# Squares of a head's rotated channels join its other channels before the statistics matmuls of a two-layer hybrid trunk

## The chip, the cores and the metric

The kernel runs on one core of a Trainium2 chip. The metric is device time in microseconds (us) of one execution. Before the change it took 756.54 us, the median of three runs (756.30, 756.54 and 756.56 us). One further execution was recorded by the hardware profiler; all durations below come from it.

A core has five engines with a queue each, and every queue runs in order: TensorE (PE, matrix products; its weight loads are shown as PEld), VectorE (DVE), ScalarE (ACT), GpSimd (POOL) and SyncE (SP, which here issues nearly all DMAs). Engines wait for each other through semaphores.

## The reference

Two layers. Each normalizes the residual stream, projects it, runs a causal pooling mixer and a latent attention side by side, and adds both back. The lines that matter here are the normalizations (D_MODEL 1024, 512 tokens behind 16 meta tokens, so 528 in all; 8 heads with 64 plain and 32 rotated channels):

```python
def rmsnorm(x, gain):
    xf = x.astype(jnp.float32)
    inv = lax.rsqrt(jnp.mean(xf * xf, axis=-1, keepdims=True) + NORM_EPS)
    return (xf * inv * gain.astype(jnp.float32)).astype(x.dtype)

def mla(c_q_raw, c_kv_raw, k_rope_raw, pos, ...):
    c_q = rmsnorm(c_q_raw, g_qa)
    c_kv = rmsnorm(c_kv_raw, g_kva)
    q = (c_q @ w_q_b).reshape(B, L, N_HEADS, QK_HEAD_DIM)
    ...
    k = jnp.concatenate([k_nope, k_pe], axis=-1)
    q = rmsnorm(q, g_qn)
    k = rmsnorm(k, g_kn)
    q = jnp.concatenate([q[..., :64], apply_rope(q[..., 64:], pos)], axis=-1)
    k = jnp.concatenate([k[..., :64], apply_rope(k[..., 64:], pos)], axis=-1)
    o = causal_block_attention(q, k, v)

# in each layer
    h = rmsnorm(h_res, norm_gain[l])
    proj = h @ w_in[l]          # u, z, c_q, c_kv, k_rope, z_mla, g_pool, g_mla
```

So each layer needs the sum of squares of a token over the 1024 channels of the stream, over the 256 channels of `c_kv`, and, for every head, over the 96 channels of its query and of its key.

## The kernel before

Activations lie transposed: channels on the 128 partitions, tokens along the free axis. FULL is the two halves of 264 tokens; the last layer works on the 512 real tokens (XTOK) where it can, so its products are 512 wide. Every f32 product is made of three matmuls (`mm3`, lines 205 to 207: high by high, high by low, low by high), with weights split into a high part on ACT (`whi`, line 200) and a low part on DVE (`wlo`, line 201). Three weight buffers rotate. The projections form one list of products, the main stream; a Python clock (`clk`, nanoseconds of matmul columns) says where in this stream the rest of the program is written: `fill_now(ns)` writes about so many nanoseconds of main stream first. A scheduler then sets the final order on each engine. PE runs what stands in its queue in order, so the main stream is the cover for all that the other engines do.

Sums over channels, which lie on partitions, are matmuls with a thin stationary operand. Two places make them:

- `norm_sums` (line 426): squares of `c_kv` (tiles `csq`, two of 128 channels) and, in the second layer, squares of the stream (tiles `xsq`, eight, already added on POOL to two by `square_x`, line 382) against a 128x32 block of ones. Each matmul uses a quarter of the array's columns (`tile_position=(0, g)`, g = 0, 32, 64, 96), so four of them make one round. In the first layer the sums over the stream come from rows of `x` instead (line 400). The sums go by DMA to DRAM (line 438 or 440) and come back folded on 16 partitions (line 448); `newton` makes reciprocal square roots, which go out and come back spread over the partitions as `rinv` and `cinv` (line 465).
- `stat` and `stat_go` (line 535): squares of keys, queries, the shared rotated key (`kr_rest`) and an epsilon row (`acc`, C_CQ) against 128x16 selector columns of `cst`, which choose the head. All wait for the last square of the batch. Before, a layer has 24: 8 for keys, 2 for the rotated key, 2 for `acc`, 4 for the queries' rotated channels (`qr`, two tiles with the rotated channels of four heads each), 8 for the queries' other channels (`qn`, four tiles with two heads each). `stat_rows` (lines 543 and 544) evacuates, and `qk_stats` goes on to the factors of queries and keys, `kdr` in DRAM and the broadcasts `bc`, from which `keys` and `prep` build the operands of the heads' scores on POOL (lines 807, 809 and 811).

`q_stat` squares a half of a query tile on ACT (line 730) into a scratch half taken from `halves()`: parts of `xb`, then of `attD` and `attE`. `rope` (lines 573 to 576) rotates on DVE and POOL. `square_x` squares a tile of the new stream for the next layer.

Of the kernel before, what the change touches and what calls it, by code (L numbers as in the profile page):

```python
# [9 lines left out]
F32 = mybir.dt.float32  # L10
# [4 lines left out]
ALU = mybir.AluOpType  # L15
# [65 lines left out]
def trunk(ctx, tc, xT, xrow, mrow, pos, win, wkr, wqb, wkb, wvb, wgr, wpu, wmu, wout, gains, const, yT):  # L81
# [255 lines left out]
    scr = dp.tile([P, 8, SEQ], F32, name="scr")  # L337
    nsr = [dp.tile([4, T], F32, name=f"nsr{l}") for l in range(DEPTH)]
    ndr = [dp.tile([3, T], F32, name=f"ndr{l}") for l in range(DEPTH)]
# [8 lines left out]
    class Layer:  # L348
        def __init__(self, l):
            self.l, self.last = l, l == DEPTH - 1  # L350
            self.XS = XTOK if self.last else FULL
            self.x0 = NM if self.last else 0
            self.xt = xt if l == 0 else [None] * 8
            self.hs, self.us, self.zps = hbuf, [None] * 4, [None] * 4
            self.cs, self.cqs, self.ys, self.am = [None] * 2, [None] * 6, [None] * 4, [None] * 8
            self.kn, self.qn, self.zms, self.ogs = [None] * 4, [None] * 4, [None] * 4, [None] * 4
            self.qr, self.qf = [None] * 2, [None] * 2
            self.gms, self.mg, self.xr, self.vw = [None] * 8, [None] * 8, [None] * 8, []
            self.made = [None] * 8
            self.csq, self.xsq = [None] * 2, [None] * 8  # L360
            self.sq, self.half = [], halves()
            self.hosted = self.st = self.acc = self.inv = self.cinv = self.kraw = self.kp = None
# [13 lines left out]
        def square_x(self, k):  # L376
            self.xsq[k] = slot(f"cq{4 + k}" if k < 4 else f"q{k}")
            made = act.activation(self.xsq[k][:, :T], self.xt[k][:, :T], AF.Square)
            for w in (1, 2):
                if k % (2 * w) == 2 * w - 1:  # L380
                    d, e = self.xsq[k - 2 * w + 1], self.xsq[k + 1 - w]
                    gp.tensor_add(d[:, :T], d[:, :T], e[:, :T])
# [24 lines left out]
        def norm_sums(self):  # L407
            if self.l:
                fill_now(2600)
            else:  # L410
# [5 lines left out]
                for _ in range(9):  # L416
                    next(rows)
            px, pc = mmt() if self.l else None, mmt()
            xs = self.xsq[::4] if self.l else []
            runs = [(px, t, m, m < 2, m >= len(xs) - 2) for m, t in enumerate(xs)]  # L420
            runs += [(pc, t, m, True, True) for m, t in enumerate(self.csq)]
            for k in range(0, len(runs), 2):
                for s, (a, b) in enumerate(FULL):
                    for ps, t, m, start, stop in runs[k:k + 2]:
                        g = 64 * s + 32 * (m % 2)
                        mm = pe.matmul(ps[g:g + 32, :HALF], ones[:, 0:32], t[:, a:b], start=start, stop=stop,  # L426
                                       tile_position=(0, g))
                        if t is not self.csq[1]:
                            behind(mm, self.csq_last)
            self.kr_sums()  # L430
            sums = tmp()
            for s, (a, b) in enumerate(FULL):
                if self.l:
                    act.activation(sums[0:64, a:b], px[64 * s:64 * s + 64, :HALF], AF.Copy)
                dve.tensor_copy(sums[64:128, a:b], pc[64 * s:64 * s + 64, :HALF])
            raw, norms = nsr[self.l], ndr[self.l]
            if self.l:
                sp.dma_start(raw, sums[0:97:32, 0:T])
            else:
                sp.dma_start(raw[2:4], sums[64:97:32, 0:T])  # L440
# [5 lines left out]
            nq = sm.tile([16, 4, C], F32, tag="nq", name=nm("nq"))  # L446
# [3 lines left out]
            dve.scalar_tensor_tensor(out=na[:, 0, :], in0=nq[:, 1, :], scalar=1.0 / D, in1=na[:, 0, :],  # L450
                                     op0=ALU.mult, op1=ALU.add)
            dve.tensor_scalar(na[:, 1, :], na[:, 0, :], EPS, None, op0=ALU.mult)
            dve.tensor_scalar(ny[:, 2, :], na[:, 1, :], EPS, None, op0=ALU.mult)
            for m in range(2):
                dve.scalar_tensor_tensor(out=na[:, 1, :], in0=nq[:, 2 + m, :], scalar=1.0 / 256,
                                         in1=na[:, 1, :], op0=ALU.mult, op1=ALU.add)
            newton(ny[:, 0:2, :], na, nt)
# [266 lines left out]

        def q_stat(self, ps, a, b, c):
            for a0, b0 in FULL:
                a0, b0 = max(a, a0), min(b, b0)
                if a0 < b0:
                    q = next(self.half)
                    made = act.activation(q[:, :b0 - a0], ps[:, a0 - a:b0 - a], AF.Square)  # L730
                    self.stat(q[:, :b0 - a0], a0, b0, c, made)

        def ev_qr(self, r):
            def ev(ps, a, b):
                if a == self.x0:
                    self.qr[r] = (slot(f"q{4 + 2 * r}", F32R), slot(f"q{5 + 2 * r}", F32R))
                    self.qf[r] = slot(f"q{2 + r}")
                f = self.qf[r]
                act.activation(f[:, a:b], ps, AF.Copy, scale=self.g(G_QR))
                self.q_stat(ps, a, b, C_IR + 4 - 4 * r)  # L740

                self.rope(f[:, a:b], f[:, a:b], a, b)
                split(*self.qr[r], f[:, a:b], a, b)
            return ev

        def ev_qn(self, p):
            def ev(ps, a, b):
                if a == self.x0:
                    self.qn[p] = slot(f"q{p}")
                act.activation(self.qn[p][:, a:b], ps, AF.Copy, scale=self.g(G_QN))  # L750
                self.q_stat(ps, a, b, C_IK + 6 - 2 * p)
            return ev

        def qk_stats(self):
            fill_now(LAG + 100)
            self.stat_go()
# [36 lines left out]
        def prep(self, h):  # L793
            p, odd = h // 2, h % 2
            n0, r0 = (64, 0) if odd else (0, 64)
            kd = self.ks[p][odd]
            g0 = 32 * (h % 4)
            qh, ql = qhl[odd]
# [11 lines left out]
            for d, f in zip((qh, ql), self.qr[h // 4]):  # L810
                gp.tensor_copy(d[r0:r0 + 32, x0:T], f[g0:g0 + 32, x0:T])  # L811
            m = P if odd else QK
# [414 lines left out]
def constants():  # L1227
# [5 lines left out]
    c[64:128, C_IK + 15] = 1.0  # L1233
    for i in range(4):
        c[32 * i:32 * i + 32, C_IR + 12 + i] = 1.0
    c[0:32, C_KPE:C_KPE + 8] = 1.0
# [12 lines left out]
def arrange(x, positions, meta_tokens, norm_gain, w_in, pool_w_group, pool_scale, pool_w_up, q_a_norm_gain,  # L1249
# [16 lines left out]
    no, ro = np.arange(64), 64 + np.arange(32)  # L1266
    cols = np.concatenate([QK * h + ro for h in range(H)] + [QK * h + no for h in range(H)])
    wqb = tiles(w_q_b[:, :, cols])
# [27 lines left out]
```

## Time and profile before

| what | value |
|---|---|
| median of three runs | 756.54 us |
| the profiled execution | 756.64 us, with a span of 754.9 us from its first to its last instruction |
| granted TensorE clock | full in all 40 slices |
| PE busy | 749.7 us, 99% of the span |
| DVE, ACT, POOL busy | 548.1, 395.9 and 218.8 us |
| statistics matmuls, line 535 | 2.80 us of the chain in each layer, at 149.3 and 528.1 us |
| norm matmuls, line 426 | 0.58 us at 24.8 us and 1.03 us at 405.3 us |

A row of the timeline gives start, duration, engine, line, operation, output and inputs, shape and count, and in brackets the idle time before it with what ended it. Matmul rows overlap, since matmuls are pipelined: the distance between starts is what one costs. An f32 matmul of lines 426, 501 and 535 shows as two records, so 8 records are 4 matmuls.

### The profile page before, as it was taken

Reading aid. Unit: us, or ns where it says so; the run is one execution under the profiler, and the core shown is the slowest. Engines: PE = TensorE matmul, PEld = TensorE weight load, DVE = VectorE, ACT = ScalarE, POOL = GpSimd, SP = SyncE. Lnnn points to the kernel's source line nnn. Section 1 sums busy time; section 2 is a strip of 40 time slices with the busy share of each in tenths; the row PEclk is TensorE's granted clock in tenths of the full one; section 3 lists DMA queues with packets and bytes.
Section 4 is the critical chain, followed back from the end, with each engine's and each line's share of the span. In section 5 each row is a group of like instructions: output and inputs, shape, how many; then the busy total and the mean of one; then the engine's idle time right before and its main releaser. Section 6 shows DMA issues by size and latency. Waiting matters only on the chain.

```text
span 754.9 us, 14329 instructions
## 1 busy us (share of the span) xinstructions
PE 749.7 (99%) x5038; PEld 682.9 (90%) x5038; DVE 548.1 (73%) x1209; ACT 395.9 (52%) x866; POOL 218.8 (29%) x267
## 2 busy tenths in 40 slices
PE   9999999999999999999999999999999999999998
PEld 8999899999999999999997898887788888888887
DVE  5588777457999988684466477676478999975942
ACT  6755655645565665542355446456345666653321
POOL 1126404204463620061130264023044435111400
PEclk9999999999999999999999999999999999999999
DMA  8532223443765567525642322234447756773472
GB/s 316 162 108 89 74 82 86 113 116 119 211 186 166 151 194 192 156 86 157 183 145 85 114 84 66 89 90 120 108 135 210 190 156 181 195 200 93 127 227 84
DMA packets 72853, 106.58 MB, mean 141 GB/s; under 512 B 14102, under 2 KB 34966, under 8 KB 72780
## 3 DMA queue, kind: packets, MB, share of 16 engines
q1 hardware_dynamic: 72636, 105.39, 47.6%
q8 instruction: 40, 0.66, 0.4%
q14 instruction: 33, 0.27, 0.1%
q10 hardware_dynamic: 144, 0.26, 0.1%
HBM read 89.76 MB, written 15.86 MB: 140 GB/s over the span
## 4 chain that ended last, share of the span: by engine, by line
PE 98%; DMA 1%; ACT 0%; SPq 0%; issue 0%; DVE 0%; ACTq 0%
PE mm L205 29%; PE mm L207 29%; PE mm L206 29%; PE S L205 2%; PE S L207 2%; PE S L206 2%; PE o L980 1%; PE o L983 1%; PE S L535 1%; PE S L881 1%; DMA attE<-pdr 1%; PE S L501 0%; DMA xb<-xT 0%; PE mm L995 0%; PE mm L426 0%
## 5 line engine op out<-in xcount | busy, mean ns | idle before, releaser
L205 PE MATMUL mm<-hh,whi 128*128 128x264 f32 (+2 forms) x1072 | 336.1, 315 | 0.6 <-ACT whi L200 0.6
L206 PE MATMUL mm<-hl,whi 128*128 128x264 f32 (+2 forms) x1072 | 336.6, 315 | 0.0
L207 PE MATMUL mm<-hh,wlo 128*128 128x264 f32 (+2 forms) x1072 | 336.4, 316 | 0.0
L201 DVE TENSOR_TENSOR wlo<-raw,whi 128x512 fp32r<-128x512 f32 (+2 forms) x238 | 173.4, 730 | 95.8 <-ACT whi L200 92.4
L200 ACT ACTIVATE whi<-raw 128x512 fp32r<-128x512 f32 (+2 forms) x238 | 142.3, 600 | 176.1 <-PE mm L206 136.4
L205 PEld LDWEIGHTS mm<-hh,whi 128*128 128x128 f32 x1072 | 201.3, 188 | 15.0 <-issue 0.8
L206 PEld LDWEIGHTS mm<-hl,whi 128*128 128x128 f32 x1072 | 201.6, 188 | 12.9
L207 PEld LDWEIGHTS mm<-hh,wlo 128*128 128x128 f32 x1072 | 200.9, 188 | 12.3
L649 POOL TENSOR_TENSOR racc<-racc,tmp 128x264 f32<-128x264 f32 (+1 forms) x15 | 14.4, 959 | 132.3 <-ACT tmp L648 132.3
L1055 POOL TENSOR_TENSOR tmp<-tmp,xb 128x264 f32<-128x264 f32 (+1 forms) x24 | 27.0, 1137 | 49.1 <-DVE tmp L1053 46.4
L833 DVE CUSTOM_DVE_ANT_0 S<-S,maskw,nqs 128x240 f32<-128x240 f32 (+4 forms) x80 | 37.8, 492 | 4.2 <-PE S L207 3.9
L811 POOL CAST qhl<-q 32x528 fp32r<-32x528 f32 (+1 forms) x32 | 25.1, 800 | 44.2 <-PE S L881 42.9
L809 POOL CAST kh<-cq 32x528 fp32r<-32x528 f32 x16 | 15.6, 976 | 69.8 <-issue 36.1
L206 PE MATMUL mm<-th,whi 128*128 128x264 f32 (+1 forms) x108 | 34.7, 321 | 0.0
L205 PE MATMUL mm<-cq,whi 128*128 128x264 f32 (+1 forms) x108 | 34.7, 321 | 0.0
L205 PE MATMUL mm<-u,whi 128*128 128x264 f32 (+1 forms) x108 | 34.6, 321 | 0.0
L206 PE MATMUL mm<-cq,whi 128*128 128x264 f32 (+1 forms) x108 | 34.5, 321 | 0.0
L207 PE MATMUL mm<-cq,wlo 128*128 128x264 f32 (+1 forms) x108 | 34.5, 321 | 0.0
L207 PE MATMUL mm<-u,wlo 128*128 128x264 f32 (+1 forms) x108 | 34.5, 319 | 0.0
L959 DVE TENSOR_TENSOR attE<-attE,th 128x640 fp32r<-128x640 f32 x32 | 26.9, 862 | 3.7 <-ACT th L958 3.7
L840 ACT ACTIVATE cq<-S,bia 128x400 f32<-128x400 f32 (+2 forms) x48 | 24.4, 511 | 9.2 <-DVE bia L894 7.7
L843 POOL COPY pm<-cq 128x16 f32<-128x16 f32 x32 | 18.2, 570 | 37.7 <-ACT cq L840 37.5
(301 smaller groups left out, 1369.5 us busy)
## 6 DMA issues: line engine op xcount, KB each, us to landing
raw<-win SPq DMA_DIRECT2D x143, 256.0 KB, 3.2
pdr<-attD SPq DMA_DIRECT2D x16, 640.0 KB, 3.7
attE<-pdr SPq DMA_DIRECT2D x64, 160.0 KB, 3.9
raw<-wout SPq DMA_DIRECT2D x32, 256.0 KB, 2.8
raw<-wpu SPq DMA_DIRECT2D x16, 256.0 KB, 2.7
raw<-wmu SPq DMA_DIRECT2D x16, 256.0 KB, 2.7
raw<-wqb SPq DMA_DIRECT2D x12, 256.0 KB, 2.6
xb<-xT SPq DMA_DIRECT2D x8, 264.0 KB, 5.5
```

What stands on the lines that cost most here:

```text
L200: act.activation(hi[:, :n], raw[:, :n], AF.Copy)
L201: dve.tensor_sub(lo[:, :n], raw[:, :n], hi[:, :n].bitcast(F32))
L205: first = pe.matmul(out, wh, xh, start=start, stop=False)
L206: pe.matmul(out, wh, xl, start=False, stop=False)
L207: newest[0] = pe.matmul(out, wl, xh, start=False, stop=stop)
L809: gp.tensor_copy(d[r0:r0 + 32, :], f[g0:g0 + 32, :])
L811: gp.tensor_copy(d[r0:r0 + 32, x0:T], f[g0:g0 + 32, x0:T])
L833: return dve.tensor_tensor_reduce(out=sv, in0=sv, in1=mask, scale=nqs[:, i, h:h + 1], scalar=3e38, op0=ALU.add, op1=ALU.min, accum_out=bia ...
L840: act.activation(pv, sv, AF.Exp, scale=-1.0, bias=bia[:, i:i + 1], accum_out=rs[:, c:c + 1])
L843: gp.tensor_copy(pm[:, i, 16 * odd:16 * odd + 16], pt[i][:, 0:NM])
L959: dve.tensor_sub(got[:, a:b], f[:, a:b], hi[:, a:b].bitcast(F32))
L1055: gp.tensor_add(t[:, :b - a], t[:, :b - a], self.am[m][:, a:b])
```

## The change

- Queries: the squares of the rotated channels (`qr`) are kept (`rsq`) and get no matmul of their own. When a `qn` tile has been squared, the 32 partitions of each of its two heads get their head's rotated squares added, on POOL for the tiles 0 to 2 and on DVE for tile 3. So that the partitions match, the rotated channels of heads 1 and 2 of each four change places (`SEAT`), in the weights' columns and in `prep`.
- Keys and tokens: in `norm_sums` the two `c_kv` squares are added to one tile on POOL, and in the second layer the two tiles of the stream's squares too (in `square_x`, the step of width 4). One PSUM tile holds all sums, and DVE alone evacuates it. The DMA to DRAM and back has a row fewer in the first layer and two fewer in the second.
- The statistics are written 600 ns of main stream later: `fill_now(LAG + 700)`.

```diff
+SEAT = (0, 2, 1, 3)
...
     def square_x(self, k):
         made = act.activation(self.xsq[k][:, :T], self.xt[k][:, :T], AF.Square)
-            for w in (1, 2):
+            for w in (1, 2, 4):
                 if k % (2 * w) == 2 * w - 1:
                     d, e = self.xsq[k - 2 * w + 1], self.xsq[k + 1 - w]
                     gp.tensor_add(d[:, :T], d[:, :T], e[:, :T])
...
-            px, pc = mmt() if self.l else None, mmt()
-            xs = self.xsq[::4] if self.l else []
-            runs = [(px, t, m, m < 2, m >= len(xs) - 2) for m, t in enumerate(xs)]
-            runs += [(pc, t, m, True, True) for m, t in enumerate(self.csq)]
-            for k in range(0, len(runs), 2):
-                for s, (a, b) in enumerate(FULL):
-                    for ps, t, m, start, stop in runs[k:k + 2]:
-                        g = 64 * s + 32 * (m % 2)
...
+            ps, c = mmt(), self.csq[0]
+            self.csq_last = gp.tensor_add(c[:, :T], c[:, :T], self.csq[1][:, :T])
+            runs = [(self.xsq[0], 0)] * self.l + [(c, 32)]
+            for i, (a, b) in enumerate(FULL):
+                for t, m in runs:
+                    g = 64 * i + m
+                    mm = pe.matmul(ps[g:g + 32, :HALF], ones[:, 0:32], t[:, a:b], start=True, stop=True,
+                                   tile_position=(0, g))
+                    behind(mm, self.csq_last)
...
-                if self.l:
-                    act.activation(sums[0:64, a:b], px[64 * s:64 * s + 64, :HALF], AF.Copy)
-                dve.tensor_copy(sums[64:128, a:b], pc[64 * s:64 * s + 64, :HALF])
+                g = 0 if self.l else 32
+                dve.tensor_copy(sums[g:64, a:b], ps[64 * s + g:64 * s + 64, :HALF])
...
-        def q_stat(self, ps, a, b, c):
+        def q_stat(self, ps, a, b, p=None, r=None):
             for a0, b0 in FULL:
                 a0, b0 = max(a, a0), min(b, b0)
                 if a0 < b0:
-                    q = next(self.half)
-                    made = act.activation(q[:, :b0 - a0], ps[:, a0 - a:b0 - a], AF.Square)
-                    self.stat(q[:, :b0 - a0], a0, b0, c, made)
+                    q, n = next(self.half), b0 - a0
+                    made = act.activation(q[:, :n], ps[:, a0 - a:b0 - a], AF.Square)
+                    if r is not None:
+                        self.rsq[r, a0] = q
+                        continue
+                    eng = dve if p == 3 else gp
+                    for g in (0, 64):
+                        g += 32 * (p % 2)
+                        made = eng.tensor_add(q[g:g + 32, :n], q[g:g + 32, :n], self.rsq[p // 2, a0][g:g + 32, :n])
+                    self.stat(q[:, :n], a0, b0, C_IK + 6 - 2 * p, made)
...
         def qk_stats(self):
-            fill_now(LAG + 100)
+            fill_now(LAG + 700)
...
-            g0 = 32 * (h % 4)
+            g0, gq = 32 * (h % 4), 32 * SEAT[h % 4]
...
-                gp.tensor_copy(d[r0:r0 + 32, x0:T], f[g0:g0 + 32, x0:T])
+                gp.tensor_copy(d[r0:r0 + 32, x0:T], f[gq:gq + 32, x0:T])
```

The lines of the changed file lie up to five further down or two further up than those of the file before; its rows below carry its own numbers (735 is the new addition in `q_stat`, 425 the norm matmul that was 426, 809 to 816 what was 804 to 811, 571 to 574 what was 573 to 576).

POOL, first layer, from the casts of the first heads' rotated queries (`qhl`) to the first key cast (`kh`), before; `q<-q,tcos` and `q<-q,tmp` are the two steps of the rotation, on 128 partitions and 264 tokens:

```order
L811 COPY qhl_108<-q_317_1817 32x528
L811 COPY qhl_110<-q_317_1817 32x528
L575 TENSOR_TENSOR q_331_1889<-q_331_1889,tcos 128x264 x2
L576 TENSOR_TENSOR q_331_1889<-q_331_1889,tmp_1892 128x264
L576 TENSOR_TENSOR q_331_1889<-q_331_1889,tmp_1907 128x264
L809 COPY kh_2459<-cq_419_2453 32x528
```

The same place in the changed program:

```order
L816 COPY qhl_108<-q_317_1815 32x528
L816 COPY qhl_110<-q_317_1815 32x528
L573 TENSOR_TENSOR q_331_1887<-q_331_1887,tcos 128x264 x2
L735 TENSOR_TENSOR attD_1958<-attD_1958,xb 32x264 x4
L574 TENSOR_TENSOR q_331_1887<-q_331_1887,tmp_1890 128x264
L735 TENSOR_TENSOR attD_1958<-attD_1958,xb 32x264 x2
L574 TENSOR_TENSOR q_331_1887<-q_331_1887,tmp_1905 128x264
L735 TENSOR_TENSOR attD_1958<-attD_1958,xb 32x264 x2
L735 TENSOR_TENSOR attE_2077<-attE_2077,xb 32x264 x4
L814 COPY kh_2476<-cq_419_2470 32x528
```

Twelve additions stand between the rotation of the second query tile and the first key cast, six of them ahead of its last step. In the second layer all twelve stand behind the last cast of `qhl`.

DVE, first layer, around the statistics, before; `wlo` are splits of weights, line 544 the evacuation of the statistics:

```order
L304 TENSOR_TENSOR q_330_1888<-q_331_1889,q_329_1887 128x264 x2
L201 TENSOR_TENSOR wlo_2084<-raw_2081,whi_2083 128x256
L201 TENSOR_TENSOR wlo_2116<-raw_2113,whi_2115 128x512
L201 TENSOR_TENSOR wlo_2139<-raw_2136,whi_2138 128x512
L201 TENSOR_TENSOR wlo_2202<-raw_2199,whi_2201 128x512
L201 TENSOR_TENSOR wlo_2289<-raw_2286,whi_2288 128x512
L544 TENSOR_TENSOR srows<-S_747,srows 16x264
```

The same place in the changed program:

```order
L202 TENSOR_TENSOR wlo_2126<-raw_2123,whi_2125 128x512
L305 TENSOR_TENSOR q_330_1886<-q_331_1887,q_329_1885 128x264 x2
L202 TENSOR_TENSOR wlo_2153<-raw_2150,whi_2152 128x512
L735 TENSOR_TENSOR attE_2077<-attE_2077,xb 32x264 x2
L202 TENSOR_TENSOR wlo_2187<-raw_2184,whi_2186 128x512
L735 TENSOR_TENSOR attE_2077<-attE_2077,xb 32x264 x2
L202 TENSOR_TENSOR wlo_2246<-raw_2243,whi_2245 128x512
L542 TENSOR_TENSOR srows<-S_745,srows 16x264
```

The four additions for query tile 3 stand between the last splits ahead of the statistics, and the rotation's split (`q<-q,q`) stands two weight splits later.

PE, second layer, the norm matmuls (`cq`, `q<-...,ones`) with the last product ahead and the rotated key's sums behind (`S<-xb,kn`), before:

```order
L207 MATMUL mm_5780<-hh_18_158,wlo_5777 128x512
L426 MATMUL mm_5805<-cq_853_5133,ones 32x264
L426 MATMUL mm_5805<-q_892_5392,ones 32x264
L426 MATMUL mm_5805<-cq_853_5133,ones 32x264
L426 MATMUL mm_5805<-q_892_5392,ones 32x264
L426 MATMUL mm_5806<-q_937_5684,ones 32x264
L426 MATMUL mm_5806<-q_948_5755,ones 32x264
L426 MATMUL mm_5806<-q_937_5684,ones 32x264
L426 MATMUL mm_5806<-q_948_5755,ones 32x264
L501 MATMUL S_5816<-xb,kn_926_5629 32x264 x8
```

and in the changed program:

```order
L208 MATMUL mm_5791<-hh_18_158,wlo_5788 128x512
L425 MATMUL mm_5816<-cq_853_5143,ones 32x264
L425 MATMUL mm_5816<-q_937_5695,ones 32x264
L425 MATMUL mm_5816<-cq_853_5143,ones 32x264
L425 MATMUL mm_5816<-q_937_5695,ones 32x264
L499 MATMUL S_5823<-xb,kn_926_5640 32x264 x8
```

Of eight matmuls four are left. In the first layer two of four are left, and three matmuls of the main stream moved from behind to ahead of them. Of the 24 statistics matmuls of a layer 20 are left; ahead of them stand 9 more matmuls of 264 columns in the first layer and 5 more of 512 in the second. From there on the order in the heads differs in many places on every engine, by some matmuls of main stream more or less between the same two steps.

More of the change, by code (lines that the diff above doesn't have):

```diff
@@ L337, in trunk @@
     scr = dp.tile([P, 8, SEQ], F32, name="scr")
-    nsr = [dp.tile([4, T], F32, name=f"nsr{l}") for l in range(DEPTH)]
+    nsr = [dp.tile([3 - l, T], F32, name=f"nsr{l}") for l in range(DEPTH)]
     ndr = [dp.tile([3, T], F32, name=f"ndr{l}") for l in range(DEPTH)]
@@ L1233, in constants @@
     c[64:128, C_IK + 15] = 1.0
-    for i in range(4):
-        c[32 * i:32 * i + 32, C_IR + 12 + i] = 1.0
     c[0:32, C_KPE:C_KPE + 8] = 1.0
@@ L1266, in arrange @@
     no, ro = np.arange(64), 64 + np.arange(32)
-    cols = np.concatenate([QK * h + ro for h in range(H)] + [QK * h + no for h in range(H)])
+    cols = np.concatenate([QK * (h - h % 4 + SEAT[h % 4]) + ro for h in range(H)] + [QK * h + no for h in range(H)])
     wqb = tiles(w_q_b[:, :, cols])
```

27 lines of the change are left out of this document (12 added, 15 removed).

## The prediction

> **What bounds the kernel now.** I read the page's first and fourth parts first: how busy each engine is, and the chain that ended last.
>
> ```profile
> span 754.9 us, 14329 instructions
> PE 749.7 (99%) x5038; PEld 682.9 (90%) x5038; DVE 548.1 (73%) x1209; ACT 395.9 (52%) x866; POOL 218.8 (29%) x267
> PE 98%; DMA 1%; ACT 0%; SPq 0%; issue 0%; DVE 0%; ACTq 0%
> ```
>
> PE is busy 749.7 of 754.9 us and makes 98% of the chain. Next I asked where the missing 5.2 us lie, by the table of stretches (length, then PE busy with its count):
>
> ```profile
> 0.00:6.00 6.00, 4.69 (x22) 4.30 (x22) 1.69 (x5) 3.49 (x7) 3.57 (x15) 1.00 0.65 234
> 6.00:58.00 52.00, 51.38 (x435) 49.51 (x434) 36.21 (x80) 33.49 (x77) 6.97 (x10) 1.00 0.56 187
> 290.00:292.00 2.00, 1.95 (x15) 1.69 (x15) 2.00 (x5) 1.80 (x4) 0.00 (x0) 1.00 0.80 317
> 531.00:700.00 169.00, 169.00 (x803) 140.55 (x803) 139.73 (x330) 93.66 (x208) 53.21 (x75) 1.00 0.58 164
> 700.00:755.00 55.00, 51.73 (x247) 42.80 (x246) 28.23 (x39) 12.94 (x21) 7.94 (x5) 1.00 0.46 147
> ```
>
> The idle time is 1.3 us at the start, 0.6 us before 58 us, a sliver near 291 us and 3.3 us behind the last product. The heads of the second layer (531 to 700) have none. So what leaves PE's queue shortens the kernel, and what goes to other engines costs only if PE must wait for it. The four stretches of the chain that the change touches, with their counts of records:
>
> ```profile
> 24.81 0.58 PE mm L426 x8
> 149.32 2.80 PE S L535 x48
> 405.28 1.03 PE mm L426 x16
> 528.08 2.80 PE S L535 x46
> ```
>
> How such matmuls share the array is in PE's timeline:
>
> ```profile
> 405.21 0.41 PE L426 MATMUL mm<-cq,ones 128*32 128x264 f32 x1
> 405.22 0.41 PE L426 MATMUL mm<-q,ones 128*32 128x264 f32 x1
> 405.22 0.41 PE L426 MATMUL mm<-cq,ones 128*32 128x264 f32 x1
> 405.23 0.41 PE L426 MATMUL mm<-q,ones 128*32 128x264 f32 x1
> 405.46 0.39 PE L426 MATMUL mm<-cq,ones 128*32 128x264 f32 x1
> ```
>
> Four start within 0.02 us, and the second record of each follows 0.24 us later. The unit of cost is the round of four, not the matmul: 1.03 - 0.58 = 0.45 us for the second round of line 426; at line 535, with the same 0.13 us of entry, (2.80 - 0.13) / 6 = 0.45 us.
>
> **The change part by part.**
>
> *Statistics (line 535).* From 24 to 20 matmuls, six rounds to five, in each layer: -0.45 us twice, -0.90 us. By single matmuls it would be 4 x 2.80 / 24 = 0.47 us each, so the bounds nearly meet.
>
> *Norm sums, second layer.* From 8 to 4 matmuls, two rounds to one: -0.45 us.
>
> *Norm sums, first layer.* From 4 matmuls to 2, which is half a round. The two use different columns and run side by side as the four did, so I take 0. If half of 0.58 us went it would be -0.29; more than that cannot go, and nothing is added to PE.
>
> *Additions ahead of the norm sums.* POOL adds 128x528 once more in the first layer and twice in the second. The same form is there (line 382), and the squares that it waits for end early:
>
> ```profile
> L382 POOL TENSOR_TENSOR q<-q,q 128x528 f32<-128x528 f32 x3 | 4.8, 1584 | 9.1 <-ACT q L378 9.1
> 21.72 0.66 ACT L485 ACTIVATE q<-mm 128x264 f32<-128x264 f32 x2
> 401.48 0.39 ACT L485 ACTIVATE q<-mm 128x264 f32<-128x264 f32 x1 [0.79 <-DVE kl L483]
> ```
>
> First layer: ready at 22.38 + 1.58 = 24.0 us, wanted at 24.81 us or later. Second: 401.87 + 1.58 = 403.5, wanted at 405.28. Both are hidden by the main stream that PE still has queued; 0.8 and 1.8 us are the slack, and 0 the cost.
>
> *Additions for the queries (24 on POOL, 8 on DVE).* No row shows a POOL addition on 32 partitions. The nearest are a 32-partition copy of one input and two-input forms on 128 partitions, all of 264 columns:
>
> ```profile
> L515 POOL COPY kp<-kp 32x264 f32<-32x264 f32 x12 | 6.2, 520 | 8.1 <-DVE kp L513 7.6
> L576 POOL TENSOR_TENSOR q<-q,tmp 128x264 f32<-128x264 f32 x4 | 3.6, 910 | 0.5 <-DVE tmp L574 0.4
> L576 POOL TENSOR_TENSOR kp<-kn,tmp 128x264 f32<-128x264 f32 x4 | 4.3, 1087 | 1.5 <-DVE tmp L574 1.3
> ```
>
> Between 0.52 and 1.09 us; I take 0.91, the row from the same place with the same neighbours. Twelve are 10.9 us of POOL a layer. When they can start and must end:
>
> ```profile
> 134.38 1.93 POOL L576 TENSOR_TENSOR q<-q,tmp 128x264 f32<-128x264 f32 x2
> 142.06 0.40 ACT L730 ACTIVATE attE<-mm 128x264 f32<-128x264 f32 x1
> 146.43 0.40 ACT L730 ACTIVATE attE<-mm 128x264 f32<-128x264 f32 x1
> 514.34 1.71 POOL L811 CAST qhl<-q 32x512 fp32r<-32x512 f32 x2
> 519.52 0.65 ACT L730 ACTIVATE attE<-mm 128x248 f32<-128x248 f32 x2
> 522.76 0.65 ACT L730 ACTIVATE attE<-mm 128x248 f32<-128x248 f32 x2
> ```
>
> First layer: POOL is free for them from 134.4, where the two last rotation steps stood, so 14 x 0.91 us end at 147.1. Statistics stood at 149.32; with nine more matmuls ahead, at 0.12 us (51.38 / 435 in the stretch from 6 to 58), they stand at 150.4. Slack 3.3 us. Second layer: from 516.05, 12 x 0.91 us end at 527.0; statistics at 528.08 and five wider matmuls, at 0.21 us (169.00 / 803), so at 529.1. Slack 2.1 us. The additions for tile 3 wait for squares that end at 146.8 and 523.4 and are two to four DVE steps of 0.4 us. Cost 0, covered by the main stream; the cover ends at 1.1 us an addition in both layers ((150.4 - 134.4) / 14 and (529.1 - 516.05) / 12).
>
> Who waits behind them: the rotation's last steps on POOL come four and six additions later, at 139.0 and 141.7, and the splits of that query tile (line 303 on ACT) have moved behind the square that began at 142.06, so ACT does not wait. The next POOL work is the first heads' key casts, 20 us later (one is quoted below, at 173.55).
>
> *DVE beside a busy POOL.* The same split of 128x256, with POOL in its casts and with POOL idle:
>
> ```profile
> 131.72 0.84 DVE L201 TENSOR_TENSOR wlo<-raw,whi 128x256 fp32r<-128x256 f32 x1
> 140.14 0.43 DVE L201 TENSOR_TENSOR wlo<-raw,whi 128x256 fp32r<-128x256 f32 x1 [0.92 <-ACT whi L200]
> 141.84 0.69 DVE L201 TENSOR_TENSOR wlo<-raw,whi 128x512 fp32r<-128x512 f32 x1 [1.28 <-ACT whi L200]
> 144.72 0.69 DVE L201 TENSOR_TENSOR wlo<-raw,whi 128x512 fp32r<-128x512 f32 x1 [2.18 <-ACT whi L200]
> ```
>
> The splits between 134 and 147 us (and 516 to 527) may take twice as long; DVE idles 0.9 to 2.2 us before such a split, so PE does not see it. The reverse, POOL held up by DVE, is a rival below.
>
> *Later statistics, same heads.* One step of main stream moves ahead of the statistics, the scores of the first head keep their place, so the way from statistics to scores loses about 0.5 us in the first layer. The operand that the scores need was there early:
>
> ```profile
> 173.55 0.99 POOL L807 CAST kh<-kh 64x528 fp32r<-64x528 f32 x1
> 176.71 0.60 PE L205 MATMUL S<-kh,qhl 96*128 96x272 f32 x3
> ```
>
> 2.2 us between its end and its use: 0.5 fits, cost 0. ACT's two evacuations of norm sums (line 434) and some DMA rows go from engines that do not bound: 0.
>
> *Two holes on PE.*
>
> ```profile
> 57.06 0.28 PE L207 MATMUL mm<-kh,wlo 128*128 128x264 f32 x1
> 57.97 0.36 PE L205 MATMUL mm<-hh,whi 128*128 128x264 f32 x1 [0.62 <-ACT whi L200]
> 57.40 0.76 DVE L584 TENSOR_TENSOR u<-mm,rinv 128x264 f32<-128x264 f32 x2
> 290.80 0.28 PE L205 MATMUL mm<-hh,whi 128*128 128x264 f32 x1
> 291.13 0.50 PE L980 MATMUL o<-th,vt 128*128 128x512 f32 x1
> ```
>
> The first is named for ACT, but the first evacuation of `u` on DVE ends at 57.8, and PE goes on 0.15 us later: by the times it waits for PSUM, behind a DVE queue that is full from the norms' factors on. The change takes one small DVE step (line 455, some 0.2 us) out of that queue: -0.2 us (0 to -0.62; +0.2 if the new order there is worse). The second, about 0.2 us (290.80 + 0.12 to 291.13), waits for probabilities read back from DRAM; products stand a little differently around it: -0.1 us (0 to -0.2).
>
> *New order in the heads.* 300 us of heads run with no hole now; a new order can only add some. I take +0.1 (0 to +1).
>
> Sum: -0.90 - 0.45 - 0.2 - 0.1 + 0.1 = -1.55 us. The profiled execution took 756.64 us (1.74 us around its span), 0.1 above the median; from the median 756.54 this gives 754.99, so 755.0 us.
>
> **The rivals.**
>
> *Only the rounds (a smaller gain).* The holes stay, or the heads get one of up to 1.3 us: 756.54 - 1.35 = 755.2 up to 756.5. For it: the holes hang on DVE and DMA timing that the change scarcely touches. Against it: 300 us without a hole speak for slack in every head.
>
> *POOL late (slower).* PE, in order, stands at the statistics until the last addition is done, and with it the main stream. It decides from 1.1 us an addition. [...] If every addition took 1.3 us (1.09 and 0.2 of standing behind DVE), the first layer would end at 134.4 + 14 x 1.3 = 152.6, 2.2 us late, the second at 531.7, 2.6 us late: 756.54 - 1.55 + 4.8 = 759.8 us. Against it: 0.52 for 32 partitions, and DVE's idle time there. [...]
>
> *Everything counts (a larger gain).* The half round pays too (-0.29) and both holes close (-0.8): 756.54 - 1.35 - 1.1 = 754.1 us. Against it: four matmuls that start within 0.02 us.
>
> **How the numbers follow.** A measurement of this kernel tells 0.2% (1.5 us: below 755.03, above 758.05) from no change. Forecast, 754.4 to 755.6: 0.62, which its middle divides, 0.37 below 755.03 and 0.25 above. Larger gain, 754.0 to 754.4: 0.10. Only rounds with a new hole, 755.6 to 757: 0.15. POOL late: 0.13, of which 0.03 stays below 758.05, where only one layer is late. Faster 0.37 + 0.10 = 0.47, same 0.25 + 0.15 + 0.03 = 0.43, slower 0.10. The range 754.1 to 757.0 leaves out some 0.03 below and 0.12 above.
>
> **What would show it.** In the profile after: line 533 (formerly 535) at 2.35 us in the chain twice, line 425 at 0.58 us twice; the additions of line 735 at 0.5 to 1.1 us each, ending 2 us or more ahead of the statistics, with no wait of PE there; PE idle 4.9 us or less; the hole at 57 us at 0.4 us or less. Wrong would be: idle time of PE released by POOL, a first norm stretch of 0.3 us, or holes of over half a us in the heads.

## The result, and the profile after

The changed kernel takes 762.78 us (median of six runs, 761.53 to 764.47) against 756.55 us for the kernel before (six runs): a ratio of 1.0085, 95% interval 1.0075 to 1.0095. It is slower by 6.2 us, where 755.0 us was predicted and 757.0 was the end of the range.

The page of the changed kernel: its span, the engines, the granted clock of PE in 40 slices, and the shares of the chain. The recorded execution took 761.53 us, the shortest of the six.

```profile
span 759.7 us, 14302 instructions
PE 751.3 (99%) x5010; PEld 683.9 (90%) x5010; DVE 560.7 (74%) x1214; ACT 395.1 (52%) x864; POOL 241.6 (32%) x294
PEclk9999999999999999999999999999999999989999
PE 95%; DMA 2%; DVE 1%; issue 0%; SPq 0%; ACT 0%; ACTq 0%
```

PE has fewer instructions and yet more busy time, the clock row has an 8, and DMA and DVE have each a per cent more of the chain. The statistics and the second layer's norm sums (start, length, count of records) got shorter, as forecast, and POOL's additions last what was assumed:

```profile
24.99 0.35 PE mm L425 x2
25.33 0.02 PE S L499 x2
25.35 0.20 PE mm L425 x2
25.55 1.78 PE S L499 x30
149.58 2.36 PE S L533 x40
403.82 0.58 PE mm L425 x8
527.31 2.35 PE S L533 x37
...
L735 POOL TENSOR_TENSOR attD<-attD,xb 32x264 f32<-32x264 f32 x12 | 10.9, 906 | 0.8
L735 POOL TENSOR_TENSOR attD<-attD,xb 32x248 f32<-32x248 f32 x4 | 3.6, 889 | 0.3
```

The loss stands elsewhere. PE's waits, its timeline and its table of stretches (length, then PE, PEld, DVE, ACT, POOL busy with counts, granted clock, DMA share, GB/s) show one place in the second layer:

```profile
PE S L985 <- ACT th L963: 3.6, 1, 3.6
675.20 0.39 PE L206 MATMUL mm<-hh,whi 128*128 128x512 f32 x1
675.43 0.40 PE L207 MATMUL mm<-hl,whi 128*128 128x512 f32 x1
679.40 0.80 PE L985 MATMUL S<-th,vt 128*128 128x512 f32 x1 [3.57 <-ACT th L963]
684.27 0.63 PE L207 MATMUL mm<-hl,whi 128*128 128x512 f32 x1
684.69 0.63 PE L208 MATMUL mm<-hh,wlo 128*128 128x512 f32 x1
675.00:680.00 5.00, 1.43 (x6) 0.85 (x5) 1.25 (x1) 1.99 (x4) 1.47 (x1) 0.86 0.69 189
680.00:685.00 5.00, 4.94 (x15) 3.65 (x14) 4.48 (x7) 3.11 (x6) 0.06 (x1) 0.50 0.22 62
685.00:690.00 5.00, 5.00 (x22) 4.04 (x22) 2.35 (x4) 1.89 (x4) 0.00 (x0) 0.96 0.42 135
```

The product of head 7, the last head (`pv`, line 985), waits 3.57 us for `th`, the high part of the probabilities read back from DRAM (line 963 in `parts`). From 680 to 685 us the granted clock is 0.50: matmuls of 512 columns start 0.42 us apart (684.27 and 684.69) where they stood 0.23 us apart ahead of the hole (675.20 and 675.43). Marks in PE's timeline divide the whole difference of the two recorded executions:

| stretch, us | before | after | difference |
|---|---|---|---|
| to the first norm matmul | 24.74 | 24.91 | +0.17 |
| to the first norm matmul of the second layer | 380.47 | 378.84 | -1.63 |
| to head 7's product there | 272.50 | 275.65 | +3.15 |
| to the end of PE's work | 74.02 | 77.21 | +3.19 |
| to the end of the execution | 4.91 | 4.92 | +0.01 |
| sum | 756.64 | 761.53 | +4.89 |

The first layer is 1.6 us shorter, but not all of that is the change: the same first layer took 379.89 us in e3 and 379.71 in e10 below, whose edits of the kernel before touch only the second layer, so some 0.6 to 0.8 us of it lie between executions. In the third stretch two rounds went and a 3.6 us hole came; the fourth, in which nothing was changed, is 3.2 us longer by the slow clock.

Why `th` was late is seen on ACT. Before, in this order: the first of head 7's last three exponentials (line 840), the copies of head 6's and then of head 7's probabilities (line 958), and on PE head 7's product:

```profile
659.30 0.46 ACT L840 ACTIVATE cq<-S,bia 128x240 f32<-128x240 f32 x1 [0.19 <-DVE bia L894]
663.90 1.37 ACT L958 ACTIVATE th<-attE 128x640 fp32r<-128x640 f32 x2 [3.21 <-DMA attE<-pdr]
674.29 1.37 ACT L958 ACTIVATE th<-attE 128x640 fp32r<-128x640 f32 x2 [2.26 <-DMA attE<-pdr]
677.71 0.40 PE L980 MATMUL S<-th,vt 128*128 128x512 f32 x1
```

After, the three on ACT (lines 845 and 963):

```profile
663.70 1.37 ACT L963 ACTIVATE th<-attE 128x640 fp32r<-128x640 f32 x2 [4.42 <-DMA attE<-pdr]
665.49 0.44 ACT L845 ACTIVATE cq<-S,bia 128x240 f32<-128x240 f32 x1
677.98 1.36 ACT L963 ACTIVATE th<-attE 128x640 fp32r<-128x640 f32 x2 [5.47 <-DMA attE<-pdr]
```

Two items have changed places. ACT, in order, now waits 4.42 us for head 6's transfer, and head 7's exponentials stand behind that wait: 665.49 in place of 659.30 us. All that follows is a round trip: the transposes on DVE, the write to DRAM, four reads back. Write and reads on SP's queue, before:

```profile
662.63 0.34 SPq L906 DMA_DIRECT2D pdr<-attD  x1
668.51 1.74 SPq L915 DMA_DIRECT2D attE<-pdr  x4
```

and after:

```profile
667.55 0.33 SPq L911 DMA_DIRECT2D pdr<-attD  x1
671.18 2.75 SPq L920 DMA_DIRECT2D attE<-pdr  x4
```

4.9 us later at the write, 2.7 at the first read, 3.7 at the copy.

### The profile page after: what moved, and what is told of

It is laid out like the page before. It is cut to its first block, busy times and chain, and to the rows that moved or that the text cites. A ratio compares the mean times of both kernels' runs of the same rounds, so it can differ in the third digit from the quotient of the medians.

```text
span 759.7 us, 14302 instructions
## 1 busy us (share of the span) xinstructions
PE 751.3 (99%) x5010; PEld 683.9 (90%) x5010; DVE 560.7 (74%) x1214; ACT 395.1 (52%) x864; POOL 241.6 (32%) x294
## 4 chain that ended last, share of the span: by engine, by line
PE 95%; DMA 2%; DVE 1%; issue 0%; SPq 0%; ACT 0%; ACTq 0%
PE mm L208 28%; PE mm L206 28%; PE mm L207 28%; PE S L206 2%; PE S L207 2%; PE S L208 2%; DMA attE<-pdr 2%; PE o L985 1%; PE o L988 1%; PE S L533 1%; PE S L886 1%; DVE attE L964 1%; DMA pdr<-attD 1%; PE wps L158 1%; PE S L499 0%
## 5 line engine op out<-in xcount | busy, mean ns | idle before, releaser
L202 DVE TENSOR_TENSOR wlo<-raw,whi 128x512 fp32r<-128x512 f32 (+2 forms) x238 | 177.8, 750 | 85.8 <-ACT whi L201 81.7
L816 POOL CAST qhl<-q 32x528 fp32r<-32x528 f32 (+1 forms) x32 | 28.3, 898 | 43.2 <-PE S L886 41.9
L848 POOL COPY pm<-cq 128x16 f32<-128x16 f32 x32 | 14.4, 449 | 48.0 <-ACT cq L845 47.4
L963 ACT ACTIVATE th<-attE 128x640 fp32r<-128x640 f32 x32 | 21.8, 727 | 13.0 <-DMA attE<-pdr 9.9
```

Source lines behind the costliest of these rows:

```text
L202: dve.tensor_sub(lo[:, :n], raw[:, :n], hi[:, :n].bitcast(F32))
L816: gp.tensor_copy(d[r0:r0 + 32, x0:T], f[gq:gq + 32, x0:T])
L963: behind(act.activation(hi[:, a:b], f[:, a:b], AF.Copy), newest[0])
```

## The experiments

Theory A: the work moved off PE gives what was predicted, and the swap on ACT costs more than that. Its rivals: the moved arithmetic costs the time (B), or the new arrangement of the heads as a whole (C). Each kernel was timed against the kernel before on its own chip, whose median there was 755.9 to 756.25 us; ratios are to it.

**Is it the swap?**

e1 puts the order back in the changed kernel. `follow` sets an order and no wait; `th` collects the copies of `parts`.

```diff
-            expo(0, 0, s0, pt[0])
+            self.exps = expo(0, 0, s0, pt[0])
...
                     late = self.parts(prev)
+                    for ins in self.th:
+                        follow(ins, self.exps)
```

> The changed kernel with one order put back: in each layer the two copies of head 6's probabilities (line 963) may stand in ACT's order only behind the last exponential of head 7 (line 845), as they stood before. On PE 4 rows move, on POOL none; all of the change's arithmetic and the later statistics stay. Theory A (the swap on ACT makes head 7's probabilities late; PE runs dry before its product and its clock falls): no wait of PE at head 7's product, granted clock 1.00 from 650 to 700 us, and 756.55 - 1.55 = 755.0 us (754.5 to 755.6). Rival B (the arithmetic that was moved to POOL and DVE costs it somewhere): 762 to 763 us still. Rival C (the whole new arrangement of the heads, which the later statistics bring, and not the one swap): 762 to 763 us still, with the hole of 3.6 us at the same product or at another.

756.21 us, ratio 1.0007 (0.9995 to 1.0020). In the recorded execution (756.17 us) the clock is 1.00 from 670 to 700 us. PE's longest waits there, behind the start of the program:

```profile
PE S L987 <- ACT th L964: 0.7, 1, 0.7
PE o L987 <- ACT th L964: 0.5, 1, 0.5
```

Nearly all of the loss is gone with four moved rows on PE, which speaks against B and C. The gain did not appear: 0.7 us are still waited at the same product and 0.5 at head 6's in the first layer. And the loss is not gone from every execution: three of the twelve took 758.4 to 759.5 us, with a mean clock of 0.997 or 0.998 where the others had 0.999 or 1.000. Head 7's exponentials now start at 662.32 us, between 659.30 before and 665.49 in the changed kernel, so little slack is left.

e2 undoes the later statistics, whereupon the scheduler itself puts head 7's exponentials first:

```diff
-            fill_now(LAG + 700)
+            fill_now(LAG + 100)
```

> The changed kernel with the statistics as early as before (LAG + 100 in place of LAG + 700), everything else as changed. In its order the exponentials of head 7 stand ahead of head 6's copies again, without being told to. Theory A: 755.0 us (754.5 to 755.6), as e1, no wait of PE on POOL at the statistics since 2 us of slack remain. Rival B (the moved arithmetic): 762 to 763 us still, or more if the additions are late now. Rival C (the arrangement that the later statistics bring): 755.0 us too; this run does not tell A from C.

755.92 us, 0.9997 (0.9988 to 1.0005): no loss, but no gain in the median either. The recorded execution took 755.01 us and has no wait of PE at that product.

e3 is the kernel before with the swap alone; `exps` here holds head 7's last three exponentials:

```diff
+                    if self.last:
+                        for ins in self.exps:
+                            follow(ins, self.th[1])
```

> The kernel before with the swap alone: in the second layer the three last exponentials of head 7 (line 840 there) must stand behind the copies of head 6's probabilities (line 958 there). PE's order does not move by one row, and 3 rows each move on ACT and DVE. Theory A: the swap costs the whole difference, 762.78 - 755.0 = 7.8 us, so 756.55 + 7.8 = 764.3 us (762 to 765.5), with a wait of about 3.6 us of PE at head 7's product and a granted clock near 0.5 for some 5 us behind it. Rivals B and C: 756.5 us, within 0.3, since neither the arithmetic nor the arrangement of the heads changes.

760.31 us, 1.0060 (1.0044 to 1.0076). PE's waits and the stretches of the clock:

```profile
PE S L983 <- ACT th L960: 2.8, 1, 2.8
PE S L986 <- DVE attE L962: 0.7, 1, 0.7
680.00:685.00 5.00, 3.45 (x13) 2.69 (x14) 4.76 (x6) 3.51 (x7) 1.51 (x1) 0.78 0.09 17
685.00:690.00 5.00, 5.00 (x20) 4.01 (x20) 2.46 (x5) 2.49 (x4) 0.00 (x0) 0.88 0.51 157
```

Without any of the change's arithmetic, and with PE's order as it was, the swap costs 4.4 us. That refutes B and C as the main cause. It is less than the 7.8 expected: the hole is shorter, and the clock fell in half of the executions only. Three of the six took 760.0 to 762.2 us with a mean clock of 0.998 (the recorded one, 762.21, is one of them), the other three 759.2 to 760.6 us at 1.000.

e4 is the kernel before with `fill_now(LAG + 700)` alone.

> The kernel before with the later statistics alone (LAG + 700 in place of LAG + 100). Some 650 of PE's 4886 rows move, and on ACT head 6's copies come to stand ahead of head 7's three last exponentials, as in the changed kernel. Theory A: 764 us (762 to 765.5), the hole and the clock as in e3. Rival B: 756.5 us. Rival C: 764 us too; e1 and e3 tell it from A.

763.43 us, 1.0097 (1.0085 to 1.0109), with the swap in its order and this wait:

```profile
PE S L980 <- ACT th L958: 3.7, 1, 3.7
```

So one constant of the change brings the swap and the whole loss: 7.5 us. The changed kernel, with the same constant, loses 1.3 us less, which is near the forecast gain. Of the 3.1 us between e3 and e4 a part is the longer hole and the clock, which was 0.996 or 0.997 in all five executions of e4; that the rest of the arrangement does the remaining harm, and only together with the swap, is argued and not shown (e1 has it, and its 0.3 us above e2 are within the noise). Why 600 ns more of main stream turn these two items around in the scheduler's reckoning was not examined.

e5 leaves the swap and gives PE more to do ahead of head 7's product:

```diff
-TAIL = (9000.0, 9000.0)
+TAIL = (9000.0, 13500.0)
```

> The changed kernel, swap and later statistics included, with 21 more matmuls of the main stream (some 4.7 us at 0.22 us each) between head 7's last scores and its product in the second layer (TAIL 13500 in place of 9000 there). Theory A as e1 to e4 left it (head 7's probabilities come some 5 us late, PE has too little other work and runs dry, then its clock falls): the stall of 3.6 us and the fall of the clock go together, and the kernel comes to the level of e1 and e2, 0 to 1.4 us below the kernel before on the same chip (754.5 to 756.2). If the later product delays the output products behind it, up to 2 us more. Rival D (the late head holds up something else too, such as the output products, and the clock falls for its own reasons): 759 us or more still.

757.21 us, 1.0019 (1.0007 to 1.0032). Hole and slow clock are gone together (no wait at that product, 1.00 throughout the recorded execution, 0.999 or 1.000 in all twelve), and 5 of the 6.2 us with them. It stays 1 us above what was expected; its recorded execution has one wait more, 0.8 us at 692 us for the sum over the last two heads' outputs (line 1003), which stands behind the later product. That execution also began late, with its first norm matmul at 27.14 us (24.91 in the changed kernel), so how the 1 us divides stays open.

**What makes the clock fall?**

e9 fills the hole with matmuls of no use into a PSUM tile that nobody reads (`idle` is 18 for the last product of the second layer, otherwise 0):

```diff
+            for _ in range(idle):
+                chain(pe.matmul(d, vt[:, 0, 0, :], qhl[0][0][:, NM:T], start=True, stop=True))
             for j in range(4):
```

> The changed kernel, swap included, with 18 matmuls of no use (512 columns, 0.23 us each, into a spare tile of PSUM) chained on PE ahead of head 7's product in the second layer, where it ran dry. They fill some 4.1 us; the product still has to wait for the late probabilities until about 679.4 us. If the clock falls because PE stood idle: the granted clock stays at 1.00 behind the product and the kernel loses the idle time alone, 762.8 - 2.7 = 760.1 us (759.5 to 760.8; 2.7 is 5.8 us of matmuls at 0.43 instead of 0.23 us). If the clock falls for another reason (the transfers, or the place in the program): 762.8 us still, with a clock near 0.5 from 680 to 685 us.

763.71 us, 1.0094 (1.0079 to 1.0110): no gain, and the run does not decide, since the hole was not filled. Three main-stream matmuls that had stood between the product's first two matmuls moved behind it, and PE now waited there for the low part of the probabilities. Its waits and stretches:

```profile
PE S L991 <- DVE attE L964: 1.8, 1, 1.8
PE S L988 <- ACT th L963: 0.7, 1, 0.7
684.00:686.00 2.00, 2.00 (x9) 1.71 (x8) 0.96 (x2) 0.00 (x0) 0.00 (x0) 0.50 0.31 49
686.00:688.00 2.00, 2.00 (x8) 1.57 (x7) 0.00 (x0) 0.00 (x0) 0.00 (x0) 0.69 0.78 217
```

e12 has 20 such matmuls there, and nine more where e9 still stood idle.

> As e9, with 20 matmuls of no use ahead of head 7's product and 9 more between its first two matmuls, where PE stood idle for 1.8 us in e9 because the low part of the probabilities (line 964 on DVE) was not ready. PE's idle time between 675 and 685 us should fall from 2.5 us to 0.3 or less, but the product comes no earlier. If the clock falls because PE stood idle: the granted clock is 1.00 from 675 to 700 us, and the time is e9's less what the clock cost there, 0.6 + 1.1 = 1.7 us: 762.0 us (761.3 to 762.7). If it falls for another reason: 0.8 to 0.9 there still, and 763.5 us or more.

763.10 us, 1.0103 (1.0086 to 1.0121). The time is not what was expected, the clock is:

```profile
675.00:680.00 5.00, 4.88 (x22) 3.69 (x21) 1.01 (x1) 1.78 (x3) 1.33 (x1) 1.00 0.68 195
680.00:685.00 5.00, 5.00 (x26) 4.11 (x25) 3.44 (x5) 1.74 (x4) 0.23 (x1) 1.00 0.22 57
```

The probabilities are as late as ever (the product starts at 679.64 us), yet the clock stays at 1.00, and it is 0.999 or 1.000 in all six executions, where the changed kernel's six had 0.996 or 0.997. So the clock fell here because PE stood idle, not because of the transfers or the place. The time stays high because the 29 useless matmuls at 0.23 us take 6.7 us of PE while the useful work stands behind them. The slow stretches, at 0.50, lasted 3.4 us in e3 and e9 and 6.8 us in the changed kernel (678.57 to 685.40) and e4. The clock fell 2.7 us into the changed kernel's hole, at 678.57 us, and in e9 behind waits of 0.7 and 1.8 us.

The four recorded executions with a slow stretch also show how long PE was idle ahead of the fall. Of the last 3.41 us before it, half the length of the changed kernel's slow stretch, PE stood idle for 2.74 us (after), 1.98 (e3), some 2.8 (e4) and 2.31 (e9). In e3 the 3.41 us ahead of these held 1.22 us of the first wait, and the clock did not fall then:

```profile
675.93:679.35 3.42, 2.20 (x10) 1.46 (x8) 0.00 (x0) 0.00 (x0) 0.00 (x0) 1.00 1.08 239
679.35:682.76 3.41, 1.43 (x5) 0.86 (x5) 2.52 (x2) 3.27 (x6) 1.53 (x1) 1.00 0.33 83
```

The same program ran with a slow stretch or without one: the mean clock stayed at 1.000 in three of e3's six executions and in two of e9's four. Those were not recorded, and what set them apart is not shown.

**Where is the gain?**

e7 and e8 are the two parts of the change alone, with the statistics as early as before.

> The part on keys and tokens alone in the kernel before (squares of both key tiles and of all eight token tiles added into one tile; the queries' statistics as before). The order differs in a few rows. By the terms of the prediction -0.45 us for the round, -0.2 for the hole at 57 us: 0.4 to 0.7 us below the kernel before, no stall at head 7. If these additions cost anything: 756.5 us or more.

756.85 us, 1.0009 (1.0001 to 1.0018).

> The queries' part alone in the kernel before, with the statistics as early as before. By the terms of the prediction two rounds of 0.45 us: 0.9 us below the kernel before, less what the slack of the last product eats (0 to 0.9), no wait of PE on POOL. If the additions on POOL are late by up to 2.6 us in a layer: 757 us or more, with PE waiting at the statistics.

755.98 us, 1.0002 (0.9993 to 1.0010). Neither part shows a gain, and e7 is 0.1% slower. The executions spread widely, e7's from 755.14 to 757.81 us and e8's from 754.62 to 757.24, and the recorded ones (757.69 and 756.85) lie near the upper ends. Both have two waits at head 7's product; e7's waits and its reads on SP:

```profile
PE S L980 <- DVE attE L956: 0.8, 1, 0.8
PE S L977 <- ACT th L955: 0.7, 1, 0.7
668.40 4.18 SPq L912 DMA_DIRECT2D attE<-pdr  x4
```

The issue of the four reads took 4.18 us (4.03 in e8), against 1.74 before. The kernel before has the same round trip, and in its recorded execution PE came to the product 2.0 us after the copies had ended. If so, what is saved ahead of it is lost again where the round trip is long; the next runs test that. e6 and e10 give the last product of the second layer 2 us more main stream as cover, in e2's kernel and in the kernel before: `TAIL = (9000.0, 11000.0)`.

> The kernel of e2 (the changed one with the statistics as early as before) with 9 more matmuls of the main stream, some 2 us, ahead of head 7's product (TAIL 11000). In e2 the saving of 1.4 us was seen up to 660 us in its trace, but not in the median of its runs. If the last product's slack of 1 us (674.9 to 675.9 us in e2, 675.7 to 677.7 before) eats it in part of the executions: 1.0 to 1.5 us below the kernel before, 754.4 to 754.9 on this chip. If the saving is lost elsewhere: within 0.5 us of the kernel before.

755.06 us, 0.9992 (0.9983 to 1.0000).

> The kernel before with the same 9 matmuls more ahead of head 7's product as e6 (TAIL 11000 in the second layer). It tells what of e6's 0.9 us is the change and what is the cover. If the change's saving on PE is real and e6's cover lets it through: this one gains little, 755.6 to 756.4 us, 0.6 to 1.4 above e6. If the cover alone made e6's gain: 755.1 us, as e6.

756.02 us, 0.9998 (0.9989 to 1.0006). e11 and e13 give the cover in both layers: `TAIL = (10500.0, 11000.0)`.

> The kernel of e6 with more main stream ahead of head 7's product in the first layer too (TAIL 10500 there), where its probabilities were ready 0.3 us ahead of the product before the change. If that slack of 0.3 us costs some executions time: 0.1 to 0.5 us below e6, 754.6 to 755.0 us. If not: as e6, 755.0 to 755.2.

754.37 us, 0.9978 (0.9969 to 0.9987).

> The kernel before with the cover of e11 ahead of head 7's product in both layers (TAIL 10500 and 11000). If e11's 1.7 us are the change's own saving on PE: 1.3 to 1.6 us above e11, that is 0.998 to 1.000 of the kernel before (754.6 to 756.2 us), at most 0.4 us of it by the cover. If the cover made them: 0.9978 of the kernel before, as e11.

755.69 us, 0.9999 (0.9990 to 1.0007). The cover alone does nothing clear of noise for the kernel before. With it the change gains 0.22%, 1.7 us, on the kernel before, and 1.3 (by the medians) to 1.6 us (by the ratios) on the kernel before with cover. e11 beats both kernels. e14 and e15 are the two parts under this cover.

> The part on keys and tokens alone (as e7) under the same cover. By the terms of the prediction -0.45 us for the round in the second layer, -0.2 for the hole at 57 us and 0 for the half round in the first layer: 0.65 us below e13. The profiles say that the half round pays 0.23 us (0.58 to 0.35), which would make it 0.9 below e13. If this part costs what e7 showed: 0.5 us or more above e13.

755.36 us, 0.9990 (0.9981 to 0.9999).

> The queries' part alone with the statistics as early as before (as e8) under the same cover. By the terms of the prediction two rounds of 0.45 us: 0.9 us below e13 (0.6 to 1.1), no wait of PE on POOL. If the additions cost it what the rounds give: as e13, within 0.3 us.

755.07 us, 0.9985 (0.9976 to 0.9994). By the ratios 0.7 us for keys and tokens and 1.1 us for the queries, 1.8 together; by the medians on their chip 0.3 and 0.6 us below e13, less than was expected of each, and the first of these is within the noise (the intervals of e13 and e14 overlap). How the gain divides is read better from the marks in PE's timeline, taken as in the table above:

| kernel | first layer | to head 7's product | rest of PE's work |
|---|---|---|---|
| e13, before with cover | 379.90 | 274.57 | 71.94 |
| e14, keys and tokens | 379.26 | 274.15 | 71.92 |
| e15, queries | 378.91 | 274.18 | 71.94 |
| e11, both | 378.98 | 273.62 | 71.93 |

In the second layer the parts give 0.42 and 0.39 us, and 0.95 together: a round each, and two rounds. In the first layer the parts (0.64 and 0.99) do not add up to both together (0.92), so its column holds differences between executions too. One remark on e14's expectation: the 0.23 us for the half round were misread. In the profile after, one matmul of the rotated key's sums (the row of line 499 at 25.33 us) runs in the freed half of the round, and from the first norm matmul to the main stream behind these sums it is 2.35 us (24.99 to 27.34), against 2.36 before (24.81 to 27.17): the half round pays nothing.

## Why the prediction was wrong

The step that failed is "New order in the heads", with its +0.1 (0 to +1). It took 300 us of heads without a hole for slack in every head and bounded a new hole by 1 us. The hole measured 3.6 us in the second layer's last head, and the slow clock behind it cost some 3.2 more; holes of over half a us in the heads were among the prediction's own signs of being wrong. Three things were missed in it. The trace of before gave the slack: head 7's copies ended at 675.7 us, its product started at 677.7, and an item that changes places on ACT with a wait of 3.2 us (for head 6's copies, at 663.90) can use that up. ACT's order of the changed program shows the swap. And no rival had PE's clock in it.

"Later statistics, same heads", costed at 0, looked at the first head alone. The 600 ns shifted the heads against the main stream as a whole; e4 shows that they brought the swap, and with it all of the loss.

The other terms:

- Statistics rounds, -0.45 us twice: right. 2.80 to 2.36 and 2.35 us.
- Norm sums, second layer, -0.45: right. 1.03 to 0.58 us; e14 gives 0.42.
- Norm sums, first layer, 0: right. To the end of the rotated key's sums behind them it is 2.35 against 2.36 us.
- Additions on POOL, 0.91 us each and hidden: right. 0.906 and 0.889 us, no wait of PE at the statistics in any recorded execution. The rival *POOL late* fell. No run shows the 0.2 us of standing behind DVE that it adds to 1.09 us for each addition; the rows above have 0.906 and 0.889 us in all. The additions on DVE were taken at 0.4 us and lasted 0.43 to 0.90; in the first layer they end at 148.64 us, 0.9 us ahead of the first statistics matmul (149.51), so they are hidden with less slack than the 3.3 us reckoned for POOL's.
- Holes, -0.3 together: not settled. The first was 0.4 us after (0.62 before), but the kernel before itself shows 0.2 in e13. In the first layer e11 gained 0.92 us on e13, 0.45 of it the round; the rest could be holes or the difference between executions.

The sum, -1.55 us, is near what e11 shows: 0.9978 of 756.19 us is -1.7, and on e13 it is 1.3 to 1.6 us. It holds for the arithmetic under a cover that the prediction did not have; the rounds, -1.35 of it, are shown, and that the -0.3 for the holes fits as well may be luck. With the early statistics and no more cover (e2) the gain does not show in the median. e6, e10 and e11 show that cover ahead of head 7's product brings it out; that it was lost there for want of slack is argued from the waits of e1, e7 and e8. The median of e2 (755.92 us) lies in the range of the rival *Only the rounds*, 755.2 to 756.5, but its recorded execution has no hole in the heads such as this rival names.

## What to carry to other kernels

Where a scheduler sets the order, compare the order of the engines that feed the bound one, too, and look for an item that now stands behind another's wait: what it delays is a chain, here exponentials, transposes, a write and a read back, and the cost is that chain's lateness less the slack at its consumer. A saving on the bound engine moves it towards everything it waits for next; it counts only if the tightest of these has slack for it, and where none is left, some independent work moved ahead of the consumer gives it back. A hole on PE is to be priced with the slow clock that may come with it: here, with waits of 2.5 to 3.9 us in all at the product, 3.4 or 6.8 us at a granted clock of 0.50, which cost 3.2 us behind the changed kernel's hole of 3.6, or nothing, as in the three executions of e3 with a mean clock of 1.000.

## What the runs showed of the hardware

- The granted clock fell to 0.50 in PE's waits of 3.6 and 3.7 us (after, e4), some 2.7 to 2.8 us into them, and behind pairs of waits of 2.8 and 0.7 (e3) and 0.7 and 1.8 us (e9). It did not behind 0.7 and 0.8 us within 2.9 us (e7, 676.98 to 679.88), nor in e12, where the same lateness was filled with work. It came back to 1.00 after 3.4 us (e3, e9) or 6.8 us (after, e4). In the last two PE had again stood idle for 0.9 and 1.1 us in the first 3.4 us of the slow stretch, in the first two for at most 0.2.
- Of the 3.41 us that ended with the fall of the clock PE was idle for 2.74 us (after), 1.98 (e3), some 2.8 (e4) and 2.31 (e9). Of the 3.41 us before these in e3 it was idle for 1.22, at a clock of 1.00.
- Four reads of 160 KB on SP's queue took 1.74 to 1.88 us to issue in seven recorded executions (before, e2, e6, e11, e13, e14, e15), 2.75 to 3.40 in three (after 2.75, e9 2.81, e12 3.40), and 4.18 and 4.03 in e7 and e8, at the same place in the program. What held them was not found.
- The start differs from one execution to the next: the first norm matmul stood at 24.91 us in the changed kernel and at 27.14 us in e5, whose program is the same up to the heads of the second layer. The first layer differs too: from that matmul to the first norm matmul of the second layer it was 378.84 us in the changed kernel and 380.58 in e9, whose edit touches only the second layer. By these differences of 2.2 and 1.7 us one recorded execution does not give the median to better than a microsecond or two.
